# Compressed values as one 128-row product, and the rotary exchange of features by transfers within SBUF

## The chip, the cores and the metric

The kernel runs on one core of a Trainium2 chip. The metric is the device time of one execution in microseconds, of which the median of three runs is taken. A core has five engines that run side by side and wait for each other by semaphores: TensorE (PE; its weight loads are listed as PEld), VectorE (DVE), ScalarE (ACT), GpSimd (POOL) and SyncE (SP). Matrix products write to PSUM, everything else lies in SBUF; transfers are issued from SP's queue, one after the other in order.

## The reference, cut to what matters

Two layers of a model with 1024 tokens of width 1024. Layer 0 mixes the tokens by an mLSTM and by NSA, an attention with three branches (compressed blocks of keys, selected blocks, a window). Layer 1 mixes by an attention over 256 keys for each query, which an indexer selects. After each mixer come a norm, an MLP, a second norm and an embedding gate. Two pieces of it concern the change.

The compressed branch: keys and values of 32 tokens at a time are compressed to 63 blocks, and each query takes a softmax over them:

```python
s = jnp.einsum('bqghd,bmgd->bqghm', qb, k_cmp)
p_cmp = _masked_softmax(s, (cmp_end[None, :] <= tq[:, None])[None, :, None, None, :])
o_cmp = jnp.einsum('bqghm,bmgd->bqghd', p_cmp.astype(dt), v_cmp)
```

The rotary embedding, of the indexer's queries (32 of 64 features of a head are rotated, 16 against 16) and of the attention's queries (64 features, 32 against 32):

```python
def _rope(x, cos, sin):
    h = x.shape[-1] // 2
    c, s = cos.astype(x.dtype), sin.astype(x.dtype)
    x1, x2 = x[..., :h], x[..., h:]
    return jnp.concatenate([x1 * c - x2 * s, x1 * s + x2 * c], -1)
```

## The kernel before, in words

All products are made at the accuracy of float32 by splitting operands: ScalarE rounds a value to its high part (type float32r), VectorE or GpSimd subtracts to get the low part, and TensorE adds high times high, high times low and low times high in PSUM (`mm3`, lines 130, 133, 134). `split` (lines 94 and 95) is that pair of copy and subtraction; `wload` loads a chunk of weights and splits it (lines 107, 116, 117).

The program is one core's straight line. The order in which the instructions of each engine stand is made by a planner when the kernel is built: it simulates a timeline with priorities in the order in which the Python code issues the work, and gives every engine its list. Tuples at the head of the file (`R0`, `R1`, `ML`, `CH`) say how much of the projections is issued between the parts of an NSA block, and how the selection is spread. So SP, too, has one fixed list: loads, stores and waits stand in it in the planner's order.

**NSA, layer 0.** `nsa_block` handles 128 queries of a group of four heads; there are two groups of eight blocks, 16 calls. Group 0 runs beside the mLSTM's projections, group 1 beside its recurrence. For the compressed branch, the scores of four heads times 64 compressed keys go to `Pc` [128 queries, 4, 64]; ScalarE takes exponentials (line 712), GpSimd multiplies by gate over sum (line 716), TensorE transposes (line 719), and the transposed weights `PT` [64, 512] are split into high and low parts. Two products follow (line 723): the stationary operand is `vc`, [64 keys, high and low values side by side], the moving one first the high, then the low part of the weights. Its 128 output rows are the products with the high values (rows 0 to 63) and with the low values (64 to 127); selected and window branches add to the same PSUM tile `pv` (line 777) after transposes (line 767), and at the end of the block the two halves are added. `compress` makes `vc` once, before the blocks (line 667).

**Rotary embedding, layer 1.** Queries are made feature-major: 128 rows are the 64 features of two heads, 512 columns are tokens. `rope_feat` is called 16 times: by `index_q` four times for the first half of the tokens and four times for the second, and by `q_rope` eight times. It copies the projection out of PSUM to the tile `q` (ScalarE, line 1053), multiplies by a 128 x 128 matrix of zeros, ones and minus ones that exchanges the two halves of each head's rotated features with their signs (float32, two instructions, line 1055), multiplies that by the sines on VectorE (line 1057) and `q` by the cosines in place on GpSimd (line 1058), and adds (line 1059: VectorE in `index_q`, GpSimd in `q_rope`). `q` and `t` come from the tag `w2`, which has four buffers in this stage; the indexer's scores take theirs from there as well. The calls for the first half of the tokens stand ahead of the indexer's scores for it; those of the second half run beside the selection of blocks 2 and 3; the eight calls of `q_rope` are filling work beside the selection of blocks 4 to 7, which counts scores bit by bit on VectorE and ScalarE (lines 1389 to 1398).

Of the kernel before, what the change touches and what calls it, by code (L numbers as in the profile page):

```python
# [8 lines left out]
F32 = mybir.dt.float32  # L9
F32R = mybir.dt.float32r  # L10
# [3 lines left out]
ALU = mybir.AluOpType  # L14
# [21 lines left out]
# order of the work: what fills the tensor engine's waits, and how often  # L36
S0A = (3,)                                          # blocks counted by ScalarE while the first ones are selected
CH = (((7, 4), (6, 5)), (6, 7))                     # chains of the selection; blocks of them that ScalarE counts
R0 = ((1,) * 4,) * 6 + ((2,) * 4,) * 2              # projection steps after each part of an NSA block, group 0
R1 = ((1, 1, 1, 0),) * 8                            # the same, group 1  # L40
ML = ((), (0,), (1,), (2,), (), (3,), (4, 5), (6, 7))   # mLSTM blocks after each NSA block of group 1
DONE = 4                                            # first mLSTM block of the second half of the tokens
CG, UG = 2, 3                                       # how far exponentials may run ahead of the splits
# [4 lines left out]
class Kern:  # L48
# [53 lines left out]
    def wload(self, src, after=None, u=False):  # L102
        """a chunk of weights, split: indexed [:, 0] and [:, 1] with columns"""
# [21 lines left out]
    def mm3(self, ps, pairs, after=None):  # L125
        """pairs: list of (stationary hi, stationary lo, moving hi, moving lo); sums the products at float32's accuracy"""
# [9 lines left out]
    def lin_f(self, hT, wch, kper, width, j, half, kts=8, m=128, after=None, tag="mm"):  # L136
        """feature-major: psum [m features, 512 tokens]; wch: chunks [P, kper, width]"""
# [10 lines left out]
    def lin_t(self, hT, wch, kper, width, mb, kts=8, off=0, n=None, tag="mm", after=None):  # L148
        """token-major: psum [128 tokens of block mb, n features]"""
# [12 lines left out]
    def rstd_pow(self, out, var, n, scale=1.0):  # L162
        """out = (var*scale + eps)^-0.5, [128, n]"""
# [5 lines left out]
    def transpose_block(self, src, mb, dst):  # L169
        """src [128 tokens, 1024] -> dst[half][kg][:, k4, hi/lo, tokens]"""  # L170
# [16 lines left out]
    def ln_apply(self, z, g, b):  # L187
        """in place layer norm of z [128, 1024]"""
# [62 lines left out]
    def consts(self):  # L251
# [7 lines left out]
        # additive masks: M = zeros then the causal triangle in the last block  # L259
# [424 lines left out]
    def nsa_block(self, g, c, K, V):  # L684
# [30 lines left out]
        for hh in range(4):  # L715
            nc.gpsimd.tensor_scalar(Pc[:, hh, :], Pc[:, hh, :], st[:, 3, hh:hh + 1], 1.0, op0=ALU.mult, op1=ALU.mult)
# [879 lines left out]
```

## Time and profile before

| | |
|---|---|
| median of three runs | 3071.26 us (3067.02 to 3072.44) |
| span of the profiled execution | 3064.9 us |
| its own time | not listed; the median is 6.4 us above the span |
| TensorE busy | 2921.1 us, 95% |
| VectorE busy | 1689.3 us, 55% |
| ScalarE busy | 1126.6 us, 37% |
| GpSimd busy | 530.2 us, 17% |
| mean granted clock of TensorE | 0.98 |

A busy time is the sum of an engine's instructions, with what they wait for inside them; matmuls are pipelined, so that the distance from one start to the next says more of their price than a duration. The stages: projections and NSA to 665 us, output projection and MLP of layer 0 to about 1560, mixer of layer 1 (projections, indexer, selection, attention) to about 2220, then its MLP.

### The profile page before, as it was taken

The page shows a single profiled execution, that of the slowest core. Times are in us where ns is not written, and L with a number is a line of the kernel's source. Part 1 is how long each engine was busy: PE and PEld are TensorE (multiplying, and loading weights), DVE is VectorE, ACT ScalarE, POOL GpSimd, SP SyncE. Part 2 cuts the span into 40 slices and gives each one's busy share as a digit, 9 for nine tenths or more (in the row PEclk, how much of TensorE's full clock was granted, in tenths as well). Part 3 has the DMA queues.
Part 4 walks back from the last instruction along what each step waited for, and adds up shares of the span by engine and source line. Part 5 has one row for each costly group of instructions (what it writes and reads, how often), then busy time and mean ns, then how long its engine had stood idle before and what let it go on. Part 6 is the DMA issues. An engine that isn't in the chain of part 4 may idle for free.

```text
span 3064.9 us, 38972 instructions
## 1 busy us (share of the span) xinstructions
PE 2921.1 (95%) x14583; PEld 2447.4 (80%) x14583; DVE 1689.3 (55%) x3808; ACT 1126.6 (37%) x2136; POOL 530.2 (17%) x495
## 2 busy tenths in 40 slices
PE   9999999989999999999999787899899999999999
PEld 8878787877888888888887565789788888888887
DVE  3687678875433333334557999976453333333372
ACT  3355655642222111222334577755231122222131
POOL 0243244312100000001333323221030000000032
PEclk9999999999999999999999798999999999999999
DMA  5632433334111111111321035654511111111122
GB/s 196 186 114 69 149 121 97 107 114 154 42 55 42 55 42 55 42 55 42 122 94 35 25 110 182 246 196 138 183 43 42 55 42 55 42 55 48 50 79 86
DMA packets 136748, 280.82 MB, mean 92 GB/s; under 512 B 14320, under 2 KB 64368, under 8 KB 136304
## 3 DMA queue, kind: packets, MB, share of 16 engines
q1 hardware_dynamic: 136560, 278.34, 27.7%
q8 instruction: 115, 1.88, 0.3%
q14 instruction: 73, 0.60, 0.1%
HBM read 209.08 MB, written 69.21 MB: 91 GB/s over the span
## 4 chain that ended last, share of the span: by engine, by line
PE 77%; DVE 12%; issue 3%; DMA 3%; ACT 2%; POOL 1%; SPq 0%; POOLq 0%; DVEq 0%; ACTq 0%
PE psmm L130 21%; PE psmm L133 21%; PE psmm L134 21%; PE pss L738 1%; PE psx L777 1%; PE psx L767 1%; PE psx L178 1%; DVE PT L95 1%; DVE qk L424 1%; DVE mask L1395 1%; PE psx L1484 1%; DVE ks L1389 1%; DVE isc L1160 1%; DVE PP L740 1%; PE psx L1498 0%
## 5 line engine op out<-in xcount | busy, mean ns | idle before, releaser
L116 ACT ACTIVATE wsp<-wraw 128x1024 fp32r<-128x1024 f32 (+2 forms) x217 | 227.0, 1047 | 628.7 <-PE psmm L134 589.0
L130 PE MATMUL psmm<-wsp,hid 128*128 128x512 f32 x1024 | 399.1, 390 | 1.2 <-DVE pw L166 1.2
L133 PE MATMUL psmm<-h1T,wsp 128*128 128x512 f32 x1024 | 399.0, 390 | 0.2
L130 PE MATMUL psmm<-h1T,wsp 128*128 128x512 f32 x1024 | 398.2, 389 | 0.6 <-ACT h1T L94 0.6
L134 PE MATMUL psmm<-wsp,hid 128*128 128x512 f32 x1024 | 398.5, 389 | 0.0
L133 PE MATMUL psmm<-wsp,hid 128*128 128x512 f32 x1024 | 398.4, 389 | 0.0
L134 PE MATMUL psmm<-h1T,wsp 128*128 128x512 f32 x1024 | 398.2, 389 | 0.0
L864 DVE TENSOR_TENSOR H<-psmm,H 128x512 f32<-128x512 f32 x224 | 154.2, 689 | 296.7 <-PE psmm L134 296.6
L167 POOL TENSOR_TENSOR brs<-pw,mhalf 128x1 f32<-128x1 f32 x32 | 25.5, 797 | 1456.1 <-DVE pw L166 1456.1
L854 DVE SCALAR_TENSOR_TENSOR w<-psmm,w 128x512 f32<-128x512 f32 x128 | 88.5, 691 | 340.6 <-ACT w L853 340.6
L117 DVE TENSOR_TENSOR wsp<-wraw,wsp 128x1024 fp32r<-128x1024 f32 (+1 forms) x155 | 192.0, 1239 | 139.8 <-ACT wsp L116 136.5
L130 PEld LDWEIGHTS psmm<-wsp,hid 128*128 128x128 f32 x1024 | 192.3, 188 | 41.4 <-DVE pw L166 1.7
L130 PEld LDWEIGHTS psmm<-h1T,wsp 128*128 128x128 f32 x1024 | 192.1, 188 | 40.7 <-ACT h1T L94 1.1
L133 PEld LDWEIGHTS psmm<-h1T,wsp 128*128 128x128 f32 x1024 | 192.3, 188 | 40.5 <-DVE h1T L95 0.8
L134 PEld LDWEIGHTS psmm<-wsp,hid 128*128 128x128 f32 x1024 | 192.3, 188 | 40.0
L134 PEld LDWEIGHTS psmm<-h1T,wsp 128*128 128x128 f32 x1024 | 192.3, 188 | 39.6
L133 PEld LDWEIGHTS psmm<-wsp,hid 128*128 128x128 f32 x1024 | 192.3, 188 | 39.6
L853 ACT ACTIVATE w<-psmm 128x512 f32<-128x512 f32 x128 | 76.5, 598 | 395.4 <-PE psmm L134 395.4
L95 DVE TENSOR_TENSOR PT<-psx,PT 128x512 fp32r<-128x512 f32 (+4 forms) x272 | 155.4, 582 | 75.9 <-ACT PT L94 74.6
L94 ACT ACTIVATE PT<-psx 128x512 fp32r<-128x512 f32 (+4 forms) x272 | 135.5, 512 | 145.1 <-PE psx L767 76.5
L117 POOL TENSOR_TENSOR wsp<-wraw,wsp 128x1024 fp32r<-128x1024 f32 (+1 forms) x62 | 149.1, 2411 | 228.1 <-ACT wsp L116 211.7
L95 DVE TENSOR_TENSOR hid<-w,hid 128x512 fp32r<-128x512 f32 x128 | 88.3, 690 | 64.3 <-ACT hid L94 64.3
(475 smaller groups left out, 6325.5 us busy)
## 6 DMA issues: line engine op xcount, KB each, us to landing
wraw<-mlp_w SPq DMA_DIRECT2D x128, 512.0 KB, 3.5
wraw<-e_aqk SPq DMA_DIRECT2D x16, 512.0 KB, 4.0
pp<-pst SPq DMA_DIRECT2D x16, 512.0 KB, 3.0
wraw<-ple_gate_w SPq DMA_DIRECT2D x16, 512.0 KB, 3.8
pp<-pp SPq DMA_DIRECT2D x16, 512.0 KB, 4.1
qn<-stg SPq DMA_DIRECT2D x16, 512.0 KB, 2.9
yT<-od SPq DMA_DIRECT2D x16, 512.0 KB, 6.1
x<-x_t SPq DMA_DIRECT2D x8, 512.0 KB, 9.7
```

Source lines behind the costliest of these rows:

```text
L94: r = nc.scalar.activation(hi, src, AF.Copy)
L95: nc.vector.tensor_sub(lo, src, hi.bitcast(F32))
L116: nc.scalar.activation(sp[0], raw[:, :n], AF.Copy)
L117: eng.tensor_sub(sp[1], raw[:, :n], sp[0].bitcast(F32))
L130: m = nc.tensor.matmul(ps, wh, xh, start=(k == 0), stop=False)
L133: nc.tensor.matmul(ps, wh, xl, start=False, stop=False)
L134: nc.tensor.matmul(ps, wl, xh, start=False, stop=(k == n - 1))
L178: nc.tensor.transpose(pt[:, k * 128:(k + 1) * 128], src[:, o:o + 128], self.ident)
L424: nc.vector.scalar_tensor_tensor(out=dst, in0=raw[:, t:t + 512], scalar=cw[:, tix, t:t + 1], in1=dst, op0=ALU.mult, op1=ALU.add)
L853: nc.scalar.activation(r, ps, AF.Relu)
L854: nc.vector.scalar_tensor_tensor(out=r, in0=ps, scalar=0.0, in1=r, op0=ALU.max, op1=ALU.mult)
L864: nc.vector.tensor_add(hs, ps, hs)
```

## The change

In the compressed branch, GpSimd writes the weighted exponentials twice, side by side (`Pd`, by a broadcast input), so that the transposes give them in rows 0 to 63 and again in rows 64 to 127. ScalarE copies all 128 rows to the high part; VectorE replaces rows 64 to 127 by the low part. `vc` holds the same compressed values in both halves of its rows, for which `compress` issues the value product a second time to PSUM rows 64 to 127. One product of 128 rows then gives high plus low. `Pc` takes the buffer of the gates' tile (tag `G`, one buffer), `Pd` has one.

In the rotary embedding, the exchange of the halves is made by transfers from `q` to `t`, issued on SP's queue: for each of the two heads two of 16 rows and one of the 32 rows that aren't rotated in the indexer (six a call), or two of 32 rows (four a call). The minus sign is put into the sine tables when these are made. The matrix and its load go.

The diff without lines in which only comments or blank lines differ:

```diff
@@ compress
-                    vc = self.sm([64, 2, 64], F32R, tag=f"vc{g}", bufs=1)
-                    self.split(pk[:64, 0:64], vc[:, 0], vc[:, 1])
+                    nc.tensor.matmul(pk[64:, 0:64], y[:, g * 64:g * 64 + 64], w2[:, 0:64], start=True, stop=True)
+                    vc = self.sm([P, 2, 64], F32R, tag=f"vc{g}", bufs=1)
+                    self.split(pk[:, 0:64], vc[:, 0], vc[:, 1])
@@ nsa_block
-        Pc = self.sm([P, 4, 64], tag="npc")
+        Pc = self.sm([P, 4, 64], tag="G", bufs=1)
+        Pd = self.sm([P, 4, 2, 64], tag="npd", bufs=1)
...
-            nc.gpsimd.tensor_scalar(Pc[:, hh, :], Pc[:, hh, :], st[:, 3, hh:hh + 1], 1.0, op0=ALU.mult, op1=ALU.mult)
+            nc.gpsimd.tensor_scalar(Pd[:, hh], Pc[:, hh, :].unsqueeze(1).to_broadcast([P, 2, 64]), st[:, 3, hh:hh + 1],
+                                    1.0, op0=ALU.mult, op1=ALU.mult)
...
-            nc.tensor.transpose(pt[:64, hh * 128:hh * 128 + 128], Pc[:, hh, :], self.ident)
+            nc.tensor.transpose(pt[:, hh * 128:hh * 128 + 128], Pd[:, hh].rearrange("p a m -> p (a m)"), self.ident)
...
-        cmp_split = self.split(pt[:64], PT[:64, 0, :512], PT[:64, 1, :512])
-        for hl in range(2):
-            nc.tensor.matmul(pv, self.vc[g].rearrange("p a b -> p (a b)"), PT[:64, hl, :512], start=(hl == 0),
-                             stop=False)
+        cmp_split = nc.scalar.activation(PT[:, 0], pt, AF.Copy)
+        nc.vector.tensor_sub(PT[64:, 0], pt[64:], PT[64:, 0].bitcast(F32))
+        nc.tensor.matmul(pv, self.vc[g].rearrange("p a b -> p (a b)"), PT[:, 0], start=True, stop=False)
@@ rope_tables_feat
+        def put(dst, src, neg):
+            if neg:
+                nc.vector.tensor_scalar(dst, src, -1.0, None, op0=ALU.mult)
+            else:
+                nc.vector.tensor_copy(dst, src)
...
-                        nc.vector.tensor_copy(e[:, :, hh, 0, q * 16:q * 16 + 16], tab[:, :, 0:32:2])
+                        put(e[:, :, hh, 0, q * 16:q * 16 + 16], tab[:, :, 0:32:2], idx % 2 and not q)
...
-                        nc.vector.tensor_copy(e[:, :, hh, q, :], tab)
+                        put(e[:, :, hh, q, :], tab, idx % 2 and not q)
@@ rope_feat
-    def rope_feat(self, ps, rot, cos, sin, half, eng):
+    def rope_feat(self, ps, h, cos, sin, half, eng):
...
-        pr = self.ps("x")
-        nc.tensor.matmul(pr, rot, q, start=True, stop=True)
         t = self.w2()
-        nc.vector.tensor_mul(t, pr, sin[:, s])
+        for o in (0, 64):
+            self.load(t[o:o + h], q[o + h:o + 2 * h])
+            self.load(t[o + h:o + 2 * h], q[o:o + h])
+            if h < 32:
+                self.load(t[o + 2 * h:o + 64], q[o + 2 * h:o + 64])
+        nc.vector.tensor_mul(t, t, sin[:, s])
         nc.gpsimd.tensor_mul(q, q, cos[:, s])
@@ mixer1
-        rots = self.sm([P, 2, P], tag="rots", bufs=1)
-        self.load(rots, i["c_rot"].rearrange("a p m -> p a m"))
...
-                    q = self.rope_feat(ps, rots[:, 0], cosI, sinI, half, nc.vector)
+                    q = self.rope_feat(ps, 16, cosI, sinI, half, nc.vector)
...
-                    q = self.rope_feat(ps, rots[:, 1], cosQ, sinQ, half, nc.gpsimd)
+                    q = self.rope_feat(ps, 32, cosQ, sinQ, half, nc.gpsimd)
```

## Rows read from the trace of the kernel before

**Rows 1.** The page's part 1: busy us (share of the span) and instructions per engine.

```profile
PE 2921.1 (95%) x14583; PEld 2447.4 (80%) x14583; DVE 1689.3 (55%) x3808; ACT 1126.6 (37%) x2136; POOL 530.2 (17%) x495
```

**Rows 2.** Windows by stage: busy us of each engine, granted clock, DMA share, GB/s.

```profile
150.00:665.00 515.00, 477.99 (x3066) 417.56 (x3064) 388.72 (x1110) 300.23 (x748) 193.28 (x228) 0.96 0.34 106
...
1626.00:1700.00 74.00, 69.25 (x328) 57.01 (x329) 52.58 (x123) 36.70 (x78) 24.41 (x20) 0.98 0.10 31
1700.00:1998.00 298.00, 234.96 (x1048) 179.78 (x1047) 288.95 (x877) 207.99 (x424) 86.94 (x71) 0.90 0.42 150
```

**Rows 3.** Chain of waits, 150 to 665 us: shares of the stretch by line.

```profile
by line: PE psmm L130 8.2%; PE pss L738 8.2%; PE psmm L133 8.0%; PE psmm L134 7.8%; PE psx L777 7.8%; PE psx L767 7.5%; DVE qk L424 5.1%; issue 4.8%; DVE PP L740 3.7%; DVE PT L95 3.4%; DVE qk L429 2.2%; DMA nk<-kd 2.1%; PE psx L723 1.8%; DM
```

**Rows 4.** Timeline of TensorE: start us, us, engine, line, operation.

```profile
471.84 0.39 PE L130 MATMUL psmm<-xT,wsp 128*128 128x512 f32 x1
472.07 0.39 PE L133 MATMUL psmm<-xT,wsp 128*128 128x512 f32 x1
472.38 0.50 PE L723 MATMUL psx<-PT,vc 64*128 64x512 f32 x1
472.82 0.98 PE L767 MATMUL psx<-ident,PP 128*128 128x128 f32 x7
```

**Rows 5.** Groups of instructions, 150 to 665 us: count, busy us, mean ns, idle before.

```profile
L716 POOL TENSOR_SCALAR npc<-npc,nst 128x64 f32<-128x64 f32 x60 | 19.2, 342 | 117.0 <-DVE nst L801 74.4 <-ACT PP L750 31.7 <-DVE nst L795 10.3
...
L723 PE MATMUL psx<-PT,vc 64*128 64x512 f32 x32 | 16.4, 511 | 2.9 <-ACT PT L94 2.5 <-DVE PT L95 0.4
```

**Rows 6.** Line 667 in the compression: duration ns min/median/max.

```profile
L667 PE MATMUL psx<-fw,ny x4: 222/222/270, 115.9 to 116.1; 128*64 128x64 f32 x4
```

**Rows 7.** Tile rots: duration ns min/median/max, first and last start.

```profile
L1055 PE MATMUL psx<-w,rots x32: 590/592/697, 1638.1 to 1865.9; 128*128 128x512 f32 x32
```

**Rows 8.** Timeline of SP's queue: first and last of four issues in a row.

```profile
1587.89 0.34 SPq L82 DMA_DIRECT2D rows<-o_q_norm  x1
...
1589.23 0.43 SPq L82 DMA_DIRECT2D rows<-o_ik_b  x1
```

**Rows 9.** DMA issues: KB each, median us from issue to landing.

```profile
h<-H SPq DMA_DIRECT2D x16, 256.0 KB, 2.3
...
od<-fw SPq DMA_DIRECT2D x16, 128.0 KB, 1.7
...
fw<-e_pos SPq DMA_DIRECT2D x2, 16.0 KB, 5.1
```

**Rows 10.** Timelines, copy and sine product: the longest and the shortest of twelve waits.

```profile
1836.44 0.58 ACT L1053 ACTIVATE w<-psmm 128x512 f32<-128x512 f32 x1
...
1845.03 0.68 DVE L1057 TENSOR_TENSOR w<-psx,tab 128x512 f32<-128x512 f32 x1
...
1861.14 0.57 ACT L1053 ACTIVATE w<-psmm 128x512 f32<-128x512 f32 x1
...
1864.98 0.68 DVE L1057 TENSOR_TENSOR w<-psx,tab 128x512 f32<-128x512 f32 x1
```

**Rows 11.** Lines 1057, 1058 and 1059: duration ns min/median/max.

```profile
L1057 DVE TENSOR_TENSOR w<-psx,PT x8: 676/684/692, 1639.2 to 1734.5; 128x512 f32<-128x512 f32 x8
L1057 DVE TENSOR_TENSOR w<-psx,tab x8: 677/679/686, 1830.9 to 1870.2; 128x512 f32<-128x512 f32 x8
...
L1058 POOL TENSOR_TENSOR w<-w,PT x8: 1261/1280/1741, 1639.2 to 1731.4; 128x512 f32<-128x512 f32 x8
...
L1059 DVE TENSOR_TENSOR w<-w,w x8: 676/692/2827, 1640.5 to 1736.5; 128x512 f32<-128x512 f32 x8
```

**Rows 12.** Timelines of VectorE and GpSimd in 1640 to 1645.

```profile
1640.51 2.83 DVE L1059 TENSOR_TENSOR w<-w,w 128x512 f32<-128x512 f32 x1 [0.59 <-POOL w L1058]
1643.26 0.68 DVE L1057 TENSOR_TENSOR w<-psx,PT 128x512 f32<-128x512 f32 x1
...
1640.44 2.35 POOL L117 TENSOR_TENSOR wsp<-wraw,wsp 128x1024 fp32r<-128x1024 f32 x1
1642.75 1.74 POOL L1058 TENSOR_TENSOR w<-w,PT 128x512 f32<-128x512 f32 x1
```

More of the change, by code (lines that the diff above doesn't have):

```diff
@@ L1526, in _consts @@
     mc = np.where((16 * e + 31 <= t) & (e < 63), np.float32(0), neg).astype(np.float32).reshape(128, 512)
-    rot = np.zeros((2, 128, 128), np.float32)
-    for h in range(2):
-        for r in range(16):
-            rot[0, h * 64 + 16 + r, h * 64 + r] = -1
-            rot[0, h * 64 + r, h * 64 + 16 + r] = 1
-        for r in range(32):
-            rot[1, h * 64 + 32 + r, h * 64 + r] = -1
-            rot[1, h * 64 + r, h * 64 + 32 + r] = 1
     return {"c_ident": np.eye(128, dtype=np.float32), "c_m": m, "c_mw": mw, "c_mc": mc,
-            "c_mt": np.ascontiguousarray(tri.T), "c_valid": (q >= 31).astype(np.float32), "c_rot": rot,
+            "c_mt": np.ascontiguousarray(tri.T), "c_valid": (q >= 31).astype(np.float32),
             "c_inv": np.array(INV_FREQ, np.float32)}
```

## The prediction

> **What bounds the kernel now.** First the page's engine totals: TensorE is busy for 95% of the span, VectorE for 55% [rows 1]. That average hides different regimes, so the windows by stage come second [rows 2]. In the NSA stage (150 to 665 us, where the compressed product sits) TensorE is busy 478 of 515 us: it leads, but not alone. In 1626 to 1700, where the first four rotary calls run, TensorE is busy 69 of 74 us and VectorE 53. In 1700 to 1998, with the other twelve calls beside the selection, the roles are exchanged: VectorE 289 of 298 us, TensorE 235 at a granted clock of 0.90. So work taken from TensorE pays in the first region, hardly in the last; there, only what VectorE does or waits for counts. Third, the chain of waits over the NSA stage gives the two-product line 1.8% [rows 3].
>
> **Profiled execution and median.** The sum is made on the span of the profiled execution, 3064.9 us; the median of the runs is 3071.3, so 6.4 us lie around the span, taken as unchanged.
>
> **Compressed values, TensorE.** In each of 16 blocks two products with 64 rows go, and one with 128 comes. The trace prices one by its neighbours [rows 4]: full-height products start 0.23 us apart (471.84, 472.07); the 64-row product starts 0.31 after the one before and holds back the next by 0.44. That is 0.75 us over two steps that would otherwise take 0.46, so it occupies 0.23 + 0.29 = 0.52 us. Two cost 1.04, one of full height 0.23; the saving is 0.81 us a block, 13 us in 16 blocks. How much is on the path? The chain's 1.8% of 515 us is 9.3 us, and the line's busy time is 16.4 [rows 3, 5]: 57%, or 7.4 us. By TensorE's busy share of 93% it would be 12.1. I take 9.5, about the middle; the bounds are 0 (all of it turns into waits for VectorE and ScalarE) and 13. Four transposes a block go from 64 to 128 columns of stationary data; their moving side stays 128 columns, so 0.
>
> **Compressed values, the rest.** ScalarE's copy and VectorE's subtraction keep 512 columns, so their time stays. The product now waits for the subtraction too; before, only the second one did. GpSimd's four scalings a block double their columns: 0.34 us each now [rows 5], at most 0.34 more, 1.4 us a block. Hidden by GpSimd's idle time, 117 us before these instructions in this stage; with that cover gone it would be 22 us. The row names the wait, VectorE's factor, not GpSimd's own work: I take 0. The single buffers for Pc and Pd are read out long before the next block, 0. In the compression itself the value product is issued twice for each group: four more instructions of 0.22 us [rows 6], on a serial stretch: between 0 and 0.9, taken 0.5.
>
> **Rotary exchange, what goes.** 32 product instructions of 0.59 us, 19 us of TensorE at most [rows 7]. The 24 of the last region buy nothing while VectorE is full. The eight of 1626 to 1700 are 4.7 us; with TensorE at 94% there I credit about 2 (0 to 4.7).
>
> **Rotary exchange, what comes.** 80 transfers on SP's queue: eight calls of six, eight of four. Four in a row were issued 0.45 us apart [rows 8]. Landing of an SBUF-to-SBUF transfer is not in the trace: the nearest rows are stores of tiles, 1.7 to 2.3 us, and at the other end a 16 KB load at 5.1 [rows 9]. I take 2.3, since it is a copy of rows out of a tile with no gather. Then the last of four lands 3 x 0.45 + 2.3 = 3.6 us after ScalarE's copy (3.0 to 6.4), the last of six 4.5 us (3.9 to 7.3). Two instructions wait for it: VectorE's product with the sines, and GpSimd's product with the cosines, which overwrites what the transfers read. Behind the first stands the selection on VectorE, behind the second the sums and weight splits on GpSimd.
>
> The cover is that VectorE is late anyway. In the twelve calls after 1700 it started the sine product between 3.27 and 8.01 us after the copy ended, median 4.75; shortest and longest are shown [rows 10]. Held against 3.6 and 4.5 us, only the two shortest (3.27, and 3.52 of a six-transfer call) fall short, by 1.3 us together; at the upper landing it would be 22 us. A planner orders the queues afresh, and SP also carries stores that wait for VectorE, so I take 2. For the first four calls: they run two at a time on four w buffers, so two rounds of at most 4.5 us less the 1.2 that the two product instructions took [rows 7], 3.3 us each; bounds 0 and 6.6. I take 2, which cancels the credit of 2 above.
>
> **The sine product changes its operands.** Its input moves from PSUM to SBUF. In PSUM it took 0.68 us every time; the addition, which has both inputs in SBUF, takes 0.69 in the median but up to 2.83 [rows 11]. The timeline shows why: that addition started beside a weight split on GpSimd and ended 0.5 us after it, while a sine product from PSUM at 1643.26 ran its 0.68 us in the midst of a GpSimd product [rows 12]. After the change both products are released by the same landing, and GpSimd's is 1.28 us long [rows 11]. Bounds in the twelve calls of the full VectorE: 0 and 12 x 1.28 = 15 us. VectorE mostly arrives about a microsecond after the landing, so little of GpSimd's product is left: 0.3 us a call, 3.6 us.
>
> The Trainium skill (SBUF — State Buffer, Who interferes with whom) has this as a rule: a VectorE instruction with two SBUF inputs is locked out by a GpSimd instruction that reads SBUF, whole instruction by whole instruction. By that rule, with GpSimd always first, the term would be 15 us instead of 3.6; the addition's 2.83 us agrees with it.
>
> **Sum.** -9.5 + 0.5 - 2 + 2 + 2 + 3.6 = -3.4 us on the span: 3061.5, with the 6.4 around it 3068. A change counts as told from none beyond 0.2%, 6.1 us (below 3065.1, above 3077.4).
>
> **Rivals.**
> - *The transfers are free.* VectorE's lateness covers them all and the two products do not meet; the NSA gain stays: -9.5 + 0.5 - 2 = -11, 3060; with all 13 us realized, 3057. For it: ten of the twelve waits are longer than the landing. Against it: both products wait for one landing. Chance 0.36 (faster).
> - *Transfers late (slower).* SP issues in order; a call's transfers stand behind the store of an earlier call, which waits for VectorE's split. Then VectorE reaches the sine product before the landing and the selection stands still. From 1.1 us a call on (12 x 1.1 = 13 us) it outweighs the gain and the noise; at 2 us it is 24 - 9 + 3.6 = +19, 3090. For it: the selection holds VectorE 97% of the time, so nothing absorbs it. Against: 3.27 us of cover in the worst call. Chance 0.07.
> - *The lock at its full length (slower).* 15 in place of 3.6: +8, 3079. For it: common release; against: VectorE's usual lateness. Chance 0.07.
> - *The product saves TensorE's time but no span.* In the NSA stage other waits take it over: 0 + 0.5 + 5.6 = +6, 3077. For it: VectorE and ScalarE end TensorE's longest waits; against: the 93%. Half of it falls above the bound. Chance 0.12 (0.06 slower, 0.06 the same).
>
> The forecast, gain and price nearly equal, has 0.38. Together: faster 0.36, the same 0.44, slower 0.20. The range for 8 in 10: from 3057, where the free transfers end, to 3082, which takes in the lock and leaves out the late transfers.
>
> **What would show it.** Product: one row on the value line per block with a spacing of 0.23 us, and 150 to 665 shorter by some 9 us; wrong if TensorE's waits for PT grow as much. Transfers: landing near 2.3 us, SP's issues 0.45 us apart; wrong if VectorE's or GpSimd's idle time before the sine and cosine products is more than 4 us in all. Lock: sine products above 0.69 us, some 3.6 us over in all. The largest risk beyond these is the planner: another order on five queues, with other stretches at half clock, could move either region by several microseconds with no term above being wrong.

## The result and the profile after

The changed kernel takes 3091.6 us in the median (3088.9 to 3094.1), the kernel before 3071.6 on the same chip; the ratio is 1.0078, 95% interval 1.0064 to 1.0091. It is slower, by 20 us in the medians and 24 us by the ratio, and lies above the range forecast. The profiled execution has a span of 3092.3 us in a run of 3094.1: 1.8 us lie around a span, so most of the 6.4 us that the prediction put there was the spread of the runs.

The engine totals and the windows by stage, which answer to [rows 1] and [rows 2]:

```profile
PE 2913.1 (94%) x14539; PEld 2450.8 (79%) x14539; DVE 1699.5 (55%) x3808; ACT 1125.6 (36%) x2136; POOL 535.3 (17%) x495
```

```profile
150.00:665.00 515.00, 466.08 (x3053) 414.35 (x3051) 396.59 (x1113) 298.73 (x741) 201.59 (x235) 0.97 0.34 105
1626.00:1700.00 74.00, 64.80 (x282) 51.35 (x281) 49.28 (x101) 32.29 (x65) 24.75 (x20) 0.88 0.14 39
1700.00:1998.00 298.00, 220.49 (x962) 173.01 (x961) 280.83 (x855) 200.21 (x405) 82.89 (x62) 0.86 0.40 138
```

TensorE has 12 us less busy time in the NSA window and 19 less in the two windows of layer 1, but these windows are fixed in time and everything moved, so they hold other work too. Over the whole span its busy time falls by 8.0 us only (2921.1 to 2913.1), where the prediction took 13 and 19 us of work away. Part of the work that is left ran slower: the trace's records of the granted clock add up to 116 us at the lower of its two levels (1.2 GHz) before and 165 us after. In 1626 to 1700 the granted clock is 0.88 where it was 0.98, and in the last window VectorE, full before (289 of 298 us), has fallen to 281: there is now something that both wait for. In the chain of waits from 150 to 665 us, which answers to [rows 3], the value product (1.8% before) is not among the lines shown, which go down to 1.5%:

```profile
by line: PE psx L780 6.2%; PE psx L770 5.0%; PE pss L741 4.7%; PE psmm L130 4.1%; DVE qk L424 4.1%; PE psmm L133 4.0%; PE psmm L134 3.9%; issue 3.0%; DVE PT L95 2.6%; ACT PP L753 2.4%; DVE PP L743 1.8%; DVE qk L429 1.8%; DVE mbuf L582 1.5%;
```

Where it happened is read from the first start of two lines, the copy out of PSUM in `rope_feat` (line 1053 before, 1064 after) and the first product of the attention's scores. The groups by line, before and then after (duration in ns min/median/max, first and last start in us):

```profile
L1454 PE MATMUL pss<-K,q x96: 220/390/502, 1929.3 to 2161.2; 128*128 128x512 f32 x48, 128*128 128x128 f32 x16, 128*128 128x256 f32 x16, 128*128 128x384 f32 x16
```

```profile
L1064 ACT ACTIVATE w<-psmm x16: 572/594/600, 1641.4 to 1885.7; 128x512 f32<-128x512 f32 x16
L1466 PE MATMUL pss<-K,q x96: 220/390/500, 1955.0 to 2187.4; 128*128 128x512 f32 x48, 128*128 128x128 f32 x16, 128*128 128x256 f32 x16, 128*128 128x384 f32 x16
```

Before, the first copy started at 1634.1. So the changed kernel is 7.3 us behind when the rotary work begins, and 25.7 behind at the first score; from there to the end it only adds 1.7 (the spans of these two executions differ by 27.4). These two marks carry the experiments below: *first copy* says what layer 0 cost, *copy to score* (295.2 us before, 313.6 after) what the rotary region cost. They come from one execution a kernel. The thirteen experiments whose layer 0 stands as before have the first copy between 1628.4 and 1638.4, so a mark is good to some 5 us; verdicts go by the ratio of all runs.

The rows that the prediction asked for, all of the changed kernel. Groups of instructions by line, 150 to 665 us, which answer to [rows 5] (count, busy us, mean ns, idle before and what ended it):

```profile
L718 POOL TENSOR_SCALAR npd<-G,nst 128x128 f32<-128x128 f32 x63 | 24.0, 400 | 123.7 <-DVE nst L804 79.8 <-ACT PP L753 22.7 <-DVE nst L751 8.4
...
L727 PE MATMUL psx<-PT,vc 128*128 128x512 f32 x16 | 7.3, 454 | 6.0 <-DVE PT L726 6.0
```

The same view from 1600 to 1900 us, the sine products of the indexer's calls and of the queries' calls:

```profile
L1071 DVE TENSOR_TENSOR w<-w,PT 128x512 f32<-128x512 f32 x8 | 7.5, 932 | 11.9 <-DMA w<-w 11.8
L1071 DVE TENSOR_TENSOR w<-w,tab 128x512 f32<-128x512 f32 x8 | 5.5, 689 | 2.1 <-issue 1.2 <-DMA w<-w 0.8
```

GpSimd's cosine products of the queries' calls in the same view, before and then after:

```profile
L1058 POOL TENSOR_TENSOR w<-w,tab 128x512 f32<-128x512 f32 x8 | 11.3, 1412 | 4.6 <-PE psx L1055 4.6
```

```profile
L1072 POOL TENSOR_TENSOR w<-w,tab 128x512 f32<-128x512 f32 x8 | 12.0, 1502 | 21.4 <-DMA w<-w 19.1 <-ACT stg L94 2.0 <-ACT mask L1405 0.3
```

The transfers' issue on SP's queue (tile w: ns min/median/max) and, from the DMA issues, their size and the median us from issue to landing:

```profile
L82 SPq DMA_DIRECT2D w<-w x80: 507/588/1389, 1642.0 to 1890.6; - x80
```

```profile
w<-w SPq DMA_DIRECT2D x48, 64.0 KB, 2.0
w<-w SPq DMA_DIRECT2D x32, 32.0 KB, 1.9
```

One product a block, and ahead of it a wait of 6.0 us in all for VectorE's subtraction, for which [rows 5] had 0.4. From 150 to 665 us TensorE's waits for `PT`, by ScalarE and VectorE, go from 14.0 to 22.9 us: they grew by as much as the saving that was looked for, the sign that the prediction named. GpSimd's scaling grew by 58 ns in the mean (342 to 400), far less than the doubling allowed for. VectorE waited 11.8 us for landings in the indexer's calls, and hardly at all (0.8) in the queries' calls. There GpSimd waits: 19.1 us for landings ahead of the cosine products, where it waited 4.6 for the matrix product before. The prediction's bound for these waits was 4 us in all. The landing itself, 2.0 us, is below the 2.3 taken.

### The profile page after: what moved, and what is told of

It reads as the page before. It is cut to its first block, busy times and chain, and to the rows that moved or that the text cites. A ratio compares the mean times of both kernels' runs of the same rounds, so it can differ in the third digit from the quotient of the medians.

```text
span 3092.3 us, 39091 instructions
## 1 busy us (share of the span) xinstructions
PE 2913.1 (94%) x14539; PEld 2450.8 (79%) x14539; DVE 1699.5 (55%) x3808; ACT 1125.6 (36%) x2136; POOL 535.3 (17%) x495
## 4 chain that ended last, share of the span: by engine, by line
PE 69%; DVE 11%; DMA 3%; ACT 2%; issue 2%; SPq 1%; POOL 0%; POOLq 0%; DVEq 0%; ACTq 0%
PE psmm L130 19%; PE psmm L134 19%; PE psmm L133 19%; PE psx L178 1%; PE psx L780 1%; PE psx L770 1%; PE psx L1496 1%; PE pss L741 1%; DVE PT L95 1%; DVE isc L1172 1%; DVE qk L424 1%; DVE mask L1407 1%; SPq L82 1%; PE psx L1510 1%; PE pss L130 0%
## 5 line engine op out<-in xcount | busy, mean ns | idle before, releaser
L95 DVE TENSOR_TENSOR PT<-psx,PT 128x512 fp32r<-128x512 f32 (+3 forms) x256 | 143.6, 576 | 61.1 <-ACT PT L94 60.0
L94 ACT ACTIVATE PT<-psx 128x512 fp32r<-128x512 f32 (+3 forms) x256 | 124.9, 508 | 134.8 <-PE psx L770 77.9
```

What stands on the lines that cost most here:

```text
L94: r = nc.scalar.activation(hi, src, AF.Copy)
L95: nc.vector.tensor_sub(lo, src, hi.bitcast(F32))
```

## The experiments

Ratios are to the kernel before, run beside each on the same chip, with the 95% interval. The planner orders the queues afresh for every variant, so each ratio holds the edit together with the new order; no run keeps the order fixed.

| run | ratio | first copy | copy to score |
|---|---|---|---|
| e1_product_only | 1.0023 [1.0014, 1.0031] | 1638.7 | 298.0 |
| e2_rotary_only | 1.0067 [1.0054, 1.0080] | 1634.6 | 313.0 |
| e3_rotary_indexer | 1.0038 [1.0024, 1.0052] | 1628.4 | 305.8 |
| e4_rotary_queries | 1.0042 [1.0028, 1.0057] | 1638.4 | 306.6 |
| p1_high_only | 0.9995 [0.9986, 1.0003] | 1623.2 | 304.4 |
| p2_no_wait_for_low | 0.9993 [0.9984, 1.0002] | 1626.6 | 298.2 |
| p3_product_late | 1.0011 [1.0002, 1.0020] | 1627.0 | 298.8 |
| r5_ballast | 1.0005 [0.9996, 1.0014] | 1635.5 | 295.6 |
| r1_transfers_5w | 1.0058 [1.0045, 1.0070] | 1635.4 | 311.8 |
| r0_matrix_5w | 0.9990 [0.9981, 0.9999] | 1631.9 | 294.4 |
| r3_two_queues | 1.0072 [1.0060, 1.0085] | 1631.3 | 316.7 |
| r6_stores_off_sp | 1.0056 [1.0042, 1.0070] | 1633.2 | 318.6 |
| r7_transfers_on_pool | 1.0157 [1.0143, 1.0171] | 1633.1 | 347.5 |
| r8_transfers_and_product | 1.0029 [1.0018, 1.0041] | 1637.3 | 304.2 |
| x1_transfers_woven | 1.0030 [1.0018, 1.0042] | 1634.2 | 304.5 |
| x2_matrix_woven | 0.9987 [0.9978, 0.9996] | 1635.1 | 288.6 |
| c1_late_5w | 0.9999 [0.9990, 1.0008] | 1621.8 | 295.1 |
| c2_woven_5w | 0.9987 [0.9977, 0.9996] | 1634.8 | 286.4 |

### Which part costs

*e1_product_only*, the hunks of the change in `compress` and `nsa_block` alone:

> The compressed part of the change alone; the rotary exchange stays a matrix product. Theory A (the loss of 20 us sits in the rotary transfers, and the product's saving is eaten by new waits): between 3063 and 3077 us, no change that can be told, with TensorE's idle time ahead of the value product some 7 us on VectorE's subtraction and 5 us ahead of the transposes on GpSimd's scaling, as in the profile of the changed kernel. Theory B (any new order of the planner costs): 3080 or more here too. The prediction's own step (9 us gained): 3062.

*e2_rotary_only*, the other hunks alone:

> The rotary transfers alone; the compressed part stays two products of 64 rows. Theory A: about 3085 to 3092 us, that is 14 to 20 us above the kernel before, with the loss between 1600 and 1960 us and none before 1560. Theory B: near 3080, and loss in any stage whose order moved. The prediction's own terms for this part (-2 + 2 + 2 + 3.6): 3077.

*e3_rotary_indexer* and *e4_rotary_queries*, only one of two lines:

```diff
-                    q = self.rope_feat(ps, rots[:, 0], cosI, sinI, half, nc.vector)
+                    q = self.rope_feat_t(ps, 16, cosI, sinI, half, nc.vector)      # e3
...
-                    q = self.rope_feat(ps, rots[:, 1], cosQ, sinQ, half, nc.gpsimd)
+                    q = self.rope_feat_t(ps, 32, cosQ, sinQ, half, nc.gpsimd)      # e4
```

> Transfers in the eight calls of the indexer only (six transfers a call); the eight calls for the queries keep the matrix product, the compressed part stays as before. By the comparison of the two traces the calls for the first half of the tokens lost about 4 to 5 us between 1600 and 1680 and the queries' calls 13 to 15. Theory A expects here a loss of 4 to 6 us (3075 to 3078). Theory B expects any size, without relation to those numbers.

> Transfers in the eight calls for the queries only (four transfers a call); the indexer keeps the matrix product, the compressed part stays as before. Theory A (buffers of w are held longer, ScalarE's copy out of PSUM waits for one, TensorE for the PSUM tile, and the filling work arrives late at the attention): a loss of 10 to 15 us (3081 to 3086), visible as TensorE's idle time on ScalarE's copy between 1820 and 1960. The prediction's own view (this region is VectorE's, work of TensorE there buys or costs nothing): 3071 to 3075.

The product alone costs 0.23%, 7 us where the prediction had a gain of 9; the transfers alone 0.67%, 20 us, nearly all of the change; the indexer's and the queries' calls have about equal parts. 0.23 + 0.67 = 0.90 against 0.78 for the whole, within the intervals. e3's 12 us are twice what theory A expected of the indexer's calls (4 to 6); e4's 13 lie in its range. Whether the loss in layer 0 is the product's, or the luck of a new order on the queues, is open after these four; the next three bear on it.

### The product: its saving and its wait

*p1_high_only* and *p2_no_wait_for_low*, which leave the low part of the weights out of the product:

```diff
-        for hl in range(2):                                   # p1, on the kernel before
-            nc.tensor.matmul(pv, ..., PT[:64, hl, :512], start=(hl == 0), stop=False)
+        nc.tensor.matmul(pv, ..., PT[:64, 0, :512], start=True, stop=False)
...
-        nc.vector.tensor_sub(PT[64:, 0], pt[64:], PT[64:, 0].bitcast(F32))     # p2, on e1
+        nc.vector.tensor_sub(PT[64:, 1], pt[64:], PT[64:, 0].bitcast(F32))
```

> The kernel before with one change: of the two compressed products of a block only the one with the high part is made (the low part's product is left out; the split that makes the low part still runs, and nothing waits for it). TensorE is relieved of 16 x 0.52 = 8 us with no new wait. Theory C (the NSA stage is TensorE's, and the whole change lost its 13 us to the waits that it brought): 6 to 9 us faster than before, ratio about 0.9975. Rival D (the stage has other chains, through VectorE and ScalarE, of the same length, so that TensorE's relief of any kind turns into idle time): within 3 us of before.

> The compressed part of the change, rotary exchange by matrix, with one edit: VectorE's subtraction writes its result to a part of PT that nobody reads, so the single product of 128 rows no longer waits for it (the low part of the weights is replaced by the high part in the product). All engines have the same work as in e1_product_only, which was 6.4 us above before. Theory C: the wait for the subtraction (6 us on TensorE's queue in 150 to 640, five waits) is the cost, so 5 to 8 us below e1_product_only, at or a little below the time before. Rival D: within 3 us of e1_product_only.

*p3_product_late*: as e1, the single product issued inside the loop over branches, just ahead of the first `nc.tensor.matmul(pv[...])` of the selected branch.

> The compressed part of the change, rotary exchange by matrix, with the single product issued later: ahead of the first product of the selected branch in place of ahead of that branch's scores, so that TensorE has scores and transposes to do while VectorE subtracts. Same work as e1_product_only (1.0023 of before), where the wait for the subtraction was the cost by p2_no_wait_for_low (0.9993). If the wait is the cost and later issue hides it: 0.998 to 1.000. Rival: the weights' buffer PT is held longer and the wait moves to the later splits: 1.001 to 1.003.

TensorE's waits in 150 to 640 us (total us, times, longest) on the compressed branch and on the splits. Kernel before:

```profile
PE psx L777 <- DVE PT L95: 2.4, 6, 0.5
...
PE psx L723 <- DVE PT L95: 0.4, 1, 0.4
```

e1_product_only:

```profile
PE psx L779 <- DVE PT L95: 7.0, 12, 1.2
PE psx L726 <- DVE PT L725: 6.1, 5, 2.2
...
PE psx L722 <- POOL npd L718: 3.0, 2, 1.8
```

And the window itself, before and then e1 (length, busy us of PE first, clock 0.97 and 0.98):

```profile
150.00:640.00 490.00, 458.26 (x2934) 400.45 (x2932) 368.78 (x1049) 287.97 (x720) 186.35 (x221) 0.97 0.35 108
```

```profile
150.00:640.00 490.00, 448.03 (x2919) 397.08 (x2918) 377.75 (x1063) 287.26 (x721) 192.51 (x220) 0.98 0.35 108
```

TensorE's busy time falls by 10.2 us, and the three rows of waits rise from 2.8 to 16.1, by 13.3. The waits of the same lines on ScalarE's copies fall from 7.6 to 4.8; with them the sum rises by 10.5, about what was saved. In e1 the saving stands as idle time.

p2 takes away the wait in the second of these rows and is 0.30% below e1, 9 us: that the dependence on the subtraction costs is shown by the ratios. How it costs is less plain. The windows from the start to the first copy, before, e1, p2 and p3 (length, busy us of PE first):

```profile
0.00:1634.09 1634.09, 1574.89 (x8214) 1337.14 (x8215) 885.03 (x1986) 590.69 (x1177) 310.33 (x320) 0.99 0.29 92
```

```profile
0.00:1638.69 1638.69, 1567.15 (x8202) 1336.44 (x8203) 893.46 (x1986) 590.37 (x1177) 316.18 (x320) 0.99 0.29 92
```

```profile
0.00:1626.61 1626.61, 1557.33 (x8202) 1329.76 (x8203) 885.85 (x1986) 589.91 (x1178) 315.69 (x320) 0.99 0.29 93
```

```profile
0.00:1627.03 1627.03, 1567.16 (x8202) 1337.96 (x8203) 882.56 (x1986) 589.63 (x1178) 315.56 (x320) 0.98 0.29 93
```

TensorE's idle time (length less busy time) is 59.2 us before, 71.5 in e1, 69.3 in p2 and 59.9 in p3. So of the 12 us by which p2 reaches the first copy ahead of e1, idle time makes only 2; the other 10 are busy time, of the same instructions, and the clock was at its lower level for 31 us there in p2 and for 44 in e1. All runs say the same of the clock: its mean over the whole span is 0.980 in e1's eleven and 0.982 in p2's. The planner's order in layer 0 differs between the two as well. How the 9 us divide between the wait, the clock and the order was not separated. p2 without the wait still has 10 us more idle time than the kernel before, so other waits take most of the relief there.

p3 keeps the arithmetic and lets the wait pass behind scores and transposes. Its idle time is that of the kernel before, with 7.7 us less busy time, and its first copy is 7.1 us early: there the saving is on the path. But its ratio of 1.0011 lies in the rival's range and above the 1.000 that the wait theory allowed, so in the whole time the gain did not show.

By the ratios p1 and p3 went rival D's way or that of p3's rival, and p2 theory C's. Layer 0 rewards relief a little: 1623.2, 1626.6 and 1627.0 lie below all thirteen others, the nearest at 1628.4, closer than the 5 us that a mark is good for. None of the three ends faster than before beyond doubt, and p3 ends slower by its interval. Copy to score is 298 to 304 us in them where it was 295.2, with the code of layer 1 unchanged: the planner's order there is another one. p3's runs have a mean granted clock of 0.9785, beside 0.9817 for the kernel before on the same chip; as an estimate, twice the difference of these means times the span of 3066 us, that is 20 us more at the lower level, which is half the upper one. Whether the order gives the lead back through the clock was not tested.

### The transfers: load, buffers, queues

*r5_ballast*: matrix product kept, and beside it the transfers `x[...] <- cos[...]` into a tile that nobody reads; `junk` is laid as in the next two.

> The kernel before with its matrix product, and beside it the same 80 transfers on SP's queue at the same places, from the cosine tables to a tile that nobody reads. Nothing on VectorE or GpSimd waits for them. Theory A2 as a matter of SP's and the DMA engines' time alone (stores of the filling work and loads behind them on SP come late): 1.004 or more. Theory A4 (the cost is that the consumers wait for the transfers): within 0.1% of before, 0.999 to 1.001.

*r1_transfers_5w* and its control *r0_matrix_5w*: `w2` with five buffers, `junk` laid into the constants `Mw`, `Mc`, `MT`.

> The rotary transfers as in e2_rotary_only (compressed part as before), with five w buffers in place of four in the stage (the selection's scrap tile moves into the constants that only layer 0 reads, which makes the room). Theory A1 (a call holds its two w buffers some 2.3 us longer, two calls are in flight, and that sets the pace of the calls): the fifth buffer lets the next projection be copied out a call earlier; 8 to 15 us below e2_rotary_only, about 3073 to 3080 on a chip where before has 3067. Rival A2 (SP's queue issues the transfers late and in order, or VectorE's list stands still for a landing): within 4 us of e2_rotary_only.

> Control: the kernel before (matrix product) with the same fifth w buffer and the same room. Theory A1: a small gain or none, 0 to 5 us below before, since its calls return their buffers sooner. If it gains as much as the transfers gain from the buffer, the buffer says nothing about the transfers.

*r3_two_queues*, *r6_stores_off_sp*, *r7_transfers_on_pool*, all on e2. In their expectations theory (a) is that transfers leave late because they stand behind stores of earlier calls on SP's list, theory (b) that the exchange itself is longer:

```diff
+        for o, eng2 in ((0, nc.sync), (64, nc.scalar)):       # r3: self.load -> eng2.dma_start
...
-                    self.store(qr[wg * 2 + j][:, :, half * 512:half * 512 + 512], st.bitcast(F32))
+                    nc.gpsimd.dma_start(qr[wg * 2 + j][:, :, half * 512:half * 512 + 512], st.bitcast(F32))   # r6
...
+            nc.gpsimd.dma_start(t[o:o + h], q[o + h:o + 2 * h])       # r7: all transfers
```

> The rotary transfers as in e2_rotary_only (1.0067 of before; compressed part as before), with the transfers of the second head on ScalarE's queue and those of the first on SP's. Theory A2 (SP issues one transfer every 0.68 us and two calls are in flight: the last of twelve leaves SP 8.2 us after the first, and the sine product starts 7.9 us after the copy in place of 5.3): the series halves, and the loss shrinks by about half, 1.003 to 1.0045. Rival A3 (the landing alone and the planner's fixed lists are the cost, however short the series): 1.006 to 1.008. If ScalarE's own time for issuing hurts, above 1.008.

> The rotary transfers on SP's queue as in e2_rotary_only, with one edit: the eight stores of the queries' rotary part are issued on GpSimd's queue, so that no transfer of the queries' calls stands behind a store of an earlier call. Theory (a): the queries' share of the loss (11 to 14 us) goes, 1.003 to 1.0045. Theory (b): 1.006 to 1.007. If the stores only hold GpSimd up in place of SP: 1.006 or more, with GpSimd's waits longer.

> All 80 transfers issued on GpSimd's queue; stores and loads stay on SP. GpSimd is busy a third of that region. Theory (a): the transfers leave right after the copy; 1.002 to 1.0045. Theory (b): 1.006 or more. If issuing costs GpSimd more than SP's 0.6 us each, or its own in-order list takes SP's part: above 1.0067.

The load costs nothing that can be told: r5 moves the same bytes at the same places and stays at 1.0005. It keeps the matrix product, though, and differs from e2 in two things: nothing waits for the transfers, and TensorE has its old work between the projections. r8 below has both the waits and the product. The buffer gives 3 us with transfers and 3 without, so it isn't the hold of the w buffers (A1 falls). Two queues give nothing (A2 falls); the Trainium skill (Trainium Kernel Development and Optimization, Key Constraints) says that issuing from several queues only saves issue time, and here even that did not reach the end. The stores on SP are a real case of a transfer standing behind somebody else's wait. Timeline of SP's queue in e2, where the copy of a call ended at 1855.93:

```profile
1855.39 0.59 SPq L82 DMA_DIRECT2D qs<-qr  x1
1859.21 0.58 SPq L85 DMA_DIRECT2D qr<-stg  x1
1859.90 2.67 SPq L82 DMA_DIRECT2D w<-w  x4
```

The four transfers leave 4.0 us after the copy, right behind a store, and take 0.67 us each. But without those stores on SP (r6) the ratio is 1.0056, an interval that overlaps e2's: theory (a) is a small part at most. On GpSimd's queue it is worse (1.0157): each issue takes 0.50 us of GpSimd itself (medians 496 and 507 ns), which has the cosine products and sums of the same calls to do.

What stayed in e2, r1, r3 and r6 alike is the delay. The mean from the start of the copy to the start of the sine product, over the 16 calls of each timeline, is 5.3 us before, 7.8 in e2, 7.8 in r3, 7.9 in r6, 8.5 in r1 and 8.1 in the changed kernel. It is 7.9 in x1 and 8.1 in r8 too, at less than half of e2's loss: what the delay costs depends on what the lists hold around it.

### The series of calls

*r8_transfers_and_product*: e2 with the old product made as well, `nc.tensor.matmul(pr, rot, q, ...)`, and `pr` unread.

> The transfers as in e2_rotary_only, and the old matrix product made as well into a PSUM tile that nobody reads, 16 products of 2 x 0.59 us. Theory (c), that TensorE's lost work lets its clock fall and this is part of the price: below e2_rotary_only, 1.004 to 1.006. Theories (a) and (b): 1.0065 to 1.008, the product adds its time or nothing.

*x1_transfers_woven* (on e2) and *x2_matrix_woven* (on before):

```diff
-        fill = chain(*[q_rope(k) for k in range(2)], *[q_nope(k) for k in range(4)])
+        def weave(a, b):
+            for _ in a:
+                yield
+                for _ in range(2):
+                    next(b, None)
+                    yield
+        fill = weave(chain(*[q_rope(k) for k in range(2)]), chain(*[q_nope(k) for k in range(4)]))
```

> The rotary transfers as in e2_rotary_only, with the filling work woven: after each of the eight calls for the queries' rotary part two steps of the other queries' projections, which before all came after the eight calls. Nothing is added or left out. Theory E (the series' pace is the latency of a call, and TensorE has nothing else to do between the calls): the loss in 1820 to 1960 (11 us) goes, 1.002 to 1.004. Rival (the wait stands in VectorE's and ScalarE's lists, whatever TensorE does): 1.006 or more.

> Control: the kernel before with the same weaving, rotary exchange by the matrix product. Theory E: a shorter call leaves less to hide, so a gain of 0 to 6 us, 0.998 to 1.000; less than the transfers gain by it. If it gains as much as x1 against e2_rotary_only, the weaving says nothing about the transfers.

TensorE's timeline in e2 at the queries' projections (`psmm<-cqT,wsp`; line 1059 is the copy out of PSUM there):

```profile
1859.38 0.39 PE L134 MATMUL psmm<-cqT,wsp 128*128 128x512 f32 x1
1865.84 0.79 PE L130 MATMUL psmm<-cqT,wsp 128*128 128x512 f32 x1 [6.07 <-ACT w L1059]
...
1873.84 0.39 PE L134 MATMUL psmm<-cqT,wsp 128*128 128x512 f32 x1
...
1883.48 0.80 PE L130 MATMUL psmm<-cqT,wsp 128*128 128x512 f32 x1 [9.25 <-ACT w L1059]
```

Two projections run back to back, then TensorE stands for 6 and 9 us until ScalarE can copy one out. What holds the second copy is seen on ScalarE's list, which is in order: ahead of it stand counts of the selection, the first of which waited 4.15 us for VectorE, and the split of an earlier call:

```profile
1878.44 1.15 ACT L1400 ACTIVATE mask<-isc,ks 128x1024 bf16<-128x1024 f32 x1 [4.15 <-DVE ks L1396]
...
1881.19 1.15 ACT L1400 ACTIVATE mask<-isc,ks 128x1024 bf16<-128x1024 f32 x1
...
1882.34 0.61 ACT L94 ACTIVATE stg<-w 128x512 fp32r<-128x512 f32 x1
1882.86 0.58 ACT L1059 ACTIVATE w<-psmm 128x512 f32<-128x512 f32 x1
```

That reads as a series of eight calls, locked step by step to two other lists, whose pace is the latency of a call; and a call's exchange is now 2.5 us longer. x1 tests it. Weaving gives 0.37% with the transfers (1.0067 to 1.0030, 11 us) and 0.13% without. TensorE's waits in 1820 to 1960, e2 and then x1:

```profile
PE psmm L130 <- ACT w L1059: 18.4, 4, 9.3
PE psmm L130 <- DVE stg L99: 12.6, 4, 8.8
```

```profile
PE psmm L130 <- DVE stg L99: 12.7, 5, 5.1
PE pss L130 <- DVE stg L99: 8.1, 6, 3.1
...
PE psmm L130 <- ACT w L1059: 1.2, 2, 0.7
```

The wait on the copy goes from 18.4 to 1.2 us with the transfers' delay as it was (8.0 us from copy to sine product in x1's eight calls for the queries): theory E is borne out for the queries' part. What is left, 1.0030, is about what the indexer's calls cost alone (e3, 1.0038); they were not woven, and which wait sets their part was not found.

The end of the selection isn't what sets the time. The start of its last instruction on a mask and the first score, before, e2 and x1:

| | last mask | first score |
|---|---|---|
| before | 2009.0 | 1929.3 |
| e2_rotary_only | 2012.9 | 1947.6 |
| x1_transfers_woven | 2025.6 | 1938.7 |

In x1 the selection ends 13 us later than in e2, the scores come 9 us earlier, and the kernel is faster. r8 gains as much as x1 by a work that nobody uses. Its 1.0029 lies below every range written down for it, on the side of theory (c), the clock. The windows between the two marks, before, e2, r8 and x1:

```profile
1634.10:1929.30 295.20, 234.64 (x952) 175.11 (x951) 269.75 (x748) 195.26 (x382) 95.46 (x63) 0.91 0.28 99
```

```profile
1634.60:1947.60 313.00, 227.97 (x913) 175.07 (x912) 279.00 (x773) 200.35 (x391) 94.95 (x63) 0.84 0.32 108
```

```profile
1637.30:1941.50 304.20, 240.37 (x951) 180.59 (x950) 274.96 (x767) 198.81 (x388) 98.19 (x63) 0.87 0.34 113
```

```profile
1634.20:1938.70 304.50, 228.76 (x919) 174.53 (x918) 268.05 (x732) 192.07 (x375) 94.76 (x63) 0.87 0.33 111
```

TensorE's idle time there is 60.6 us before, 85.0 in e2, 63.8 in r8 and 75.7 in x1. So e2's loss has two parts: TensorE stands 24 us longer, and although 19 us of products went, its busy time falls by 7 only, with the granted clock at 0.84 where it was 0.91. (In e2's timeline above, the products after the two waits take 0.79 and 0.80 us, those before 0.39.) x1 takes back 9 us of idle time. In r8 the unused product stands between the projections and the wait on the copy is split into shorter ones (10.9 us in three); idle time falls by 21 us, and 12 of these come back as busy time. The clock rises to 0.87 in both, but busy time does not fall with it, so the gain of x1 and r8 over e2 is idle time first. In r8 the planner's order is another one too, and what part is that was not separated.

*c1_late_5w* and *c2_woven_5w*, combinations on the matrix version:

> The late product together with the fifth w buffer and the matrix product for the rotary exchange: the candidate to beat both kernels. If both effects stand side by side (late product 0.999, buffer 0.999): about 0.998, 6 us below before. Rival: a new order of the planner in layer 1 gives it back, as it did in p1_high_only (11 us ahead at the end of layer 0, level at the end): 0.999 to 1.002.

> The kernel before with the woven filling work and the fifth w buffer, compressed part and rotary exchange as before. If the two gains stand side by side: 0.9975 to 0.998. If they take away the same wait: 0.9985 to 0.9995.

c1 reaches the first copy 12 us early in its profiled execution, which is 7 us below the median of its runs, and ends level by the ratio; the late product adds nothing to the buffer that can be told. c2 equals x2, as expected if the buffer and the weaving take away the same wait. x2 and c2 (0.13%, 4 us) and r0 (0.10%) are the versions below both kernels: the intervals exclude 1, but the gain is below the 0.2% that the prediction called told from none.

## Why the prediction was wrong, step by step

- **Compressed values, TensorE.** Of the 13 us of work 8 show: that is what busy time up to the first copy falls by in e1 and in p3. The taken 9.5 on the path is near p3's first copy, 7.1 us early with idle time unchanged; where the product stands at its old place the same relief turns into idle time (e1, and 10 us of it in p2).
- **Compressed values, the rest: "I take 0".** This step failed. The prediction saw that the product now waits for the subtraction, and priced only GpSimd's longer scaling. The dependence costs 9 us (e1 against p2), the whole gain, and the product's part of the change measures +7 us in place of -9.5. VectorE's list is in order and 77% busy in the new window; a product that needs VectorE's subtraction has to wait its turn there. How much of the 9 us is the wait itself, and how much the clock and the order that came with it, stays open.
- **Rotary, what goes: "buy nothing while VectorE is full".** Failed with the next one. A full VectorE was taken as the end of the region, but in x1 the selection ends 13 us later than in e2 and the scores come 9 us earlier. TensorE's filling work (projections, calls, first scores) matters there: without the products its idle time between the marks grows from 60.6 to 85.0 us (e2), and of the 19 us only 7 come off its busy time, at a granted clock of 0.84 for 0.91.
- **Rotary, what comes: "the cover is that VectorE is late anyway".** Failed, and with it came most of the 20 us of e2, where the terms for the transfers added up to 5.6. The 3.27 to 8.01 us in [rows 10] were not slack that a landing can use: the sine product moved from 5.3 to 7.8 us after the copy, about as much as the exchange got longer. It stands later in VectorE's list, so VectorE hardly waits there (0.8 us); the waits show elsewhere, on GpSimd (19.1 us for landings in the queries' calls) and as TensorE's wait for ScalarE's copy (18.4 in e2, 1.2 when woven). Issue 0.67 us (taken 0.45, from short loads [rows 8]) and landing 2.0 (2.3) were sizes, and not the cause.
- **First four calls.** +2 taken; VectorE's wait for landings there is 11.8 us over all eight indexer calls where it waited 7.0 for the product before, and e3 has the indexer's calls at 0.38%, 12 us. Too small by far, and the second half of the indexer's calls had been covered by the same argument.
- **The lock of the sine product, +3.6.** It was put on the twelve calls after 1700, and there it is 0: medians 692 and 691 ns in the two groups of calls, none above 694 ns in these twelve. It fell on two of the first four calls, 1666 and 1669 ns, 2 us in all. Each of the two ends 0.55 to 0.56 us after the GpSimd cosine product beside it, which agrees with the Trainium skill's rule (SBUF — State Buffer, Who interferes with whom) that two SBUF inputs contend with GpSimd's reads.
- **Rivals.** "Product saves TensorE's time but no span" (0.12) is what came for the product. "Transfers late" at 2 us a call gave 3090, near the 3091.6, but by a mechanism that was not found, so the nearness is luck: the selection didn't stand still, and the stores on SP (r6) are a small part. The planner's new order and stretches at half clock were called the largest risk and had no term: copy to score is 3 to 9 us longer in p1 to p3, about the size that a mark is good for, and the time at the lower clock level grew from 116 to 165 us in the changed kernel.

## What to carry to other kernels

A wait measured before a change is slack only if nothing behind it sets the time; follow the result of the late instruction to its last reader before calling it cover. Work replaced by a transfer should be looked at as latency in a series: count how many calls are in flight and what the bounding engine does between them, and weave other work in, which was worth more here (11 us) than a buffer or a second queue. When work leaves an engine whose granted clock can fall, read busy time, idle time and clock before counting the work as time. When two products become one, ask what the one must now wait for; relief of a busy engine that comes with a wait for another in-order engine can be worth less than nothing, as in e1.

## What the runs showed of the hardware

Instructions of VectorE on two values a partition can take as long as GpSimd's. Timelines of e2, VectorE and then GpSimd:

```profile
1873.58 1.24 DVE L1404 TENSOR_TENSOR ks<-ks 128x2 int32<-128x2 f32 x1
1874.86 2.26 DVE L1405 SCALAR_TENSOR_TENSOR ks<-ks 128x2 int32<-128x2 int32 x1
1877.15 1.19 DVE L1396 TENSOR_SCALAR ks<-ks 128x2 int32<-128x2 int32 x1
```

```profile
1873.01 1.79 POOL L1067 TENSOR_TENSOR w<-w,tab 128x512 f32<-128x512 f32 x1 [5.56 <-DMA w<-w]
1874.77 2.33 POOL L117 TENSOR_TENSOR wsp<-wraw,wsp 128x1024 fp32r<-128x1024 f32 x1
1877.06 1.25 POOL L1068 TENSOR_TENSOR w<-w,w 128x512 f32<-128x512 f32 x1
```

Each ends within 0.05 us of the GpSimd instruction beside it, where the medians of these lines are 0.16 to 0.17 us: GpSimd holds them up, on the counting of the selection. The kernel before has it as well: its line 1389 has a median of 168 ns and a maximum of 2278. These three lines of the counting take 74.5 us there and 73.9 in e2, so it is no part of the loss. The first two have both inputs in SBUF, as in the rule above; the third has one, and which condition holds it up no run shows.

A transfer of 32 or 64 KB within SBUF landed 1.9 to 2.0 us after its issue (medians), the larger as fast as the smaller. The Trainium skill (DMA: Bandwidth & Descriptors, Anatomy of one DMA) gives about 2 us as the fixed cost on GpSimd's path, most of it for the confirmation at the end; the trace agrees for SP's queue.
